# First weights in pieces of two row tiles, the last row tile in two column halves, a norm ahead of the gates

## The chip, the cores and the metric

The program runs on one core of a Trainium2 chip. A core has TensorE (matmuls), VectorE, ScalarE, GpSimd, and SyncE, which only issues transfers; the profile calls them PE (PEld for its weight loads), DVE, ACT, POOL and SP. Each takes its own instructions in order and waits on semaphores for the others. The metric is the device time of one execution in microseconds (us), as the median of several runs.

## The reference

One layer of a hybrid decoder on 1,024 prompt tokens and 8 x 8 sample tokens, all float32:

```python
h = rms_norm(x, norm_g)                          # over D_MODEL = 1024
a, gl, zc, q, k, v, zg, lr = split(h @ w_in)     # one projection
u  = a * sigmoid(gl)                             # 512 channels
cv = silu(group_layer_norm(causal_conv31(u)))
cv = (cv @ w_pw + b_pw) * silu(zc)
o  = gated_linear_attention(q, k, v, gate(lr))   # recurrent state, exact
o  = rms_norm_per_head(o) * silu(zg)
x  = x + concat(cv, o) @ w_out
y  = rms_norm(x, final_g)
```

The conv caches and the attention states are outputs too. In what follows only the first lines (norm, the projections `gl` and `a`) and the last two (`w_out`, residual, final norm) matter.

## The kernel before

**Layout.** The 1,088 tokens lie along the free dimension, in three chunks of 384, 384 and 320 tokens (`CHUNKS` 0, 1, 2); the 1,024 model channels lie in eight row tiles of 128 partitions (`x0` to `x7`). I call the chunks first, second and third by these numbers. The third is worked on first (`FIRST = 2`).

**Products.** A float32 product is made of three fast ones: each operand is split into a high part (a copy rounded by ScalarE: `hh` of x, `h_gl` and so on of weights) and a low part (the difference, by VectorE: `hl`, `l_gl`), and high x high, high x low and low x high are summed in PSUM. So a weight half (`s_gl0_0`: four row tiles by 128 columns, 256 KB) must be loaded, copied and subtracted before TensorE can use it. One projection of one column tile and one chunk is 8 row tiles x 3 = 24 matmuls.

**The start.** The parameters (`par`) are loaded first, then row tiles of the third chunk and halves of the first four weight tiles (`gl` and `a` for column tiles 0 and 1) in turn (L1004 to L1010). For the third chunk x is not normalised before the product: `raw_split` (L504) splits x times the norm's weights, and the result is scaled afterwards by `rs`, the norm factor of each token (`gl_chunk`, `early`). `rms_scale` (L513) makes that factor: squares `sq` on ScalarE, adds on VectorE, a matmul with a constant (`ms`) that sums over partitions, logarithm and exponential on ScalarE. `rms_split` (L530) applies it and splits; the first and second chunk go that way. Sigmoids need another function table on ScalarE than logarithm and exponential; a switch is an ACT_TABLE_LOAD.

**The end.** The product with `w_out` is done in seven products of half size (a Strassen-like scheme); the last, `pr4`, adds to four PSUM banks `acc` (`ya0` to `ya3`), one for each 128 tokens. `y_first` and `y_last` finish 128 tokens: square with a sum over columns, logarithm, exponential (the factor), then the two column halves are scaled, `y` on VectorE with the final weights and `z` on ScalarE, and both are stored by SyncE.

**What sets the order.** The code only lists operations. A planner (`schedule`) simulates the engines with estimated costs and latencies and emits each engine's instructions in the order of its simulation; among ready operations the one written first goes first. `late=True` ties a transfer to the last matmul written so far. Each pool has a fixed number of slots (`wst`, the staging of weights, has 4), and a transfer waits until the work on the slot's former tile is done. Transfers go through eight semaphores in turn, so that one waits for the eighth before it.

## Time and profile before

| | |
|---|---|
| median of three runs | 468.62 us (467.6 to 469.81) |
| the profiled execution, its own time | 470.14 us |
| its span, from first to last instruction | 468.4 us |
| mean granted clock of TensorE | 0.992 |
| TensorE / VectorE / ScalarE busy | 98% / 84% / 66% |

The span is shorter than the execution's time by 1.74 us, which lies around the instructions. Busy time of TensorE alone doesn't say that it works at its peak; the granted clock says at which of its two levels it ran (1.00 is 2.4 GHz).

### The profile page before, as it was taken

What the parts mean: (1) busy time and instruction counts of PE and PEld (TensorE: products, weight loads), DVE (VectorE), ACT (ScalarE), POOL (GpSimd) and SP (SyncE); (2) the same over time, 40 slices, a digit from 0 to 9 for tenths busy, and PEclk for the clock granted to TensorE, in tenths of its full rate; (3) what the DMA queues carried; (4) which work ended last, traced back from release to release, by engine and by line L of the source; (5) the groups of instructions that cost most, each with busy time, mean ns of one, the idle gap of its engine ahead of it and who ended that gap; (6) DMA issues with size and microseconds to landing.
All of it is one profiled execution on the core that took longest, in us unless ns stands there. A gap on an engine that the chain in (4) does not pass through costs nothing.

```text
span 468.4 us, 7544 instructions
## 1 busy us (share of the span) xinstructions
PE 457.8 (98%) x2714; PEld 420.8 (90%) x2714; DVE 393.4 (84%) x627; ACT 307.6 (66%) x769; POOL 19.8 (4%) x38
## 2 busy tenths in 40 slices
PE   7999999999999999999999999999999999999993
PEld 6899989999888899898999999999999988888782
DVE  4899997999999999998999999943538948998863
ACT  6897639974633624567766677653898648879735
POOL 1000000000000000000000000000000023130000
PEclk9999999999999999999999999999999999999998
DMA  8740273141300050002211121011235393385834
GB/s 250 265 146 7 88 167 50 45 59 56 58 0 1 8 171 1 2 22 92 69 57 45 41 97 45 24 59 65 81 78 182 88 226 58 77 180 138 288 127 179
DMA packets 35477, 43.26 MB, mean 92 GB/s; under 512 B 12912, under 2 KB 19824, under 8 KB 35440
## 3 DMA queue, kind: packets, MB, share of 16 engines
q1 hardware_dynamic: 33136, 38.59, 27.2%
q0 software_dynamic: 2304, 4.20, 5.5%
q8 instruction: 21, 0.34, 0.3%
q14 instruction: 16, 0.13, 0.1%
HBM read 36.58 MB, written 6.19 MB: 91 GB/s over the span
## 4 chain that ended last, share of the span: by engine, by line
PE 89%; ACT 3%; DMA 3%; DVE 2%; SPq 1%; issue 1%; DVEq 0%
PE p_zc L409 10%; PE pv L409 10%; PE p_zg L409 10%; PE p_gl L409 10%; PE p_a L409 9%; PE ya L409 7%; PE p_q L409 5%; PE p_k L409 5%; PE pw L409 5%; PE yc L409 5%; PE po L409 2%; PE pys L409 2%; SPq L397 1%; DMA s_gl<-in_w_in 1%; PE pa L409 1%; DMA xr<-in_x 1%
## 5 line engine op out<-in xcount | busy, mean ns | idle before, releaser
L359 DVE SCALAR_TENSOR_TENSOR cv<-u,par,cv 128x1024 f32<-128x1024 f32 x120 | 151.0, 1277 | 0.2
L409 PE MATMUL p_gl<-hh,h_gl 128*128 128x384 f32 (+1 forms) x96 | 32.5, 338 | 1.9 <-ACT h_gl L353 1.0
L353 ACT ACTIVATE pr<-us,par 128x64 f32<-128x64 f32 x124 | 31.9, 341 | 1.2 <-DMA us<-in_cc 1.2
L409 PE MATMUL p_gl<-hl,h_gl 128*128 128x384 f32 (+1 forms) x96 | 31.9, 332 | 0.1
L409 PE MATMUL p_gl<-hh,l_gl 128*128 128x384 f32 (+1 forms) x96 | 32.0, 333 | 0.0
L409 PE MATMUL p_a<-hh,h_a 128*128 128x384 f32 (+1 forms) x96 | 31.9, 332 | 0.0
L409 PE MATMUL p_a<-hl,h_a 128*128 128x384 f32 (+1 forms) x96 | 31.9, 332 | 0.0
L409 PE MATMUL p_a<-hh,l_a 128*128 128x384 f32 (+1 forms) x96 | 31.6, 331 | 0.0
L409 PE MATMUL p_zc<-hl,h_zc 128*128 128x384 f32 (+1 forms) x96 | 31.6, 329 | 0.0
L409 PE MATMUL p_zc<-hh,h_zc 128*128 128x384 f32 (+1 forms) x96 | 31.5, 328 | 0.0
L409 PE MATMUL p_zc<-hh,l_zc 128*128 128x384 f32 (+1 forms) x96 | 31.4, 328 | 0.0
L409 PE MATMUL p_zg<-hh,h_zg 128*128 128x384 f32 (+1 forms) x96 | 31.3, 326 | 0.0
L409 PE MATMUL p_zg<-hl,h_zg 128*128 128x384 f32 (+1 forms) x96 | 31.3, 326 | 0.0
L409 PE MATMUL p_zg<-hh,l_zg 128*128 128x384 f32 (+1 forms) x96 | 31.3, 326 | 0.0
L409 PE MATMUL pv<-h_v,hl 128*128 128x512 f32 x64 | 24.9, 390 | 0.0
L409 PE MATMUL pv<-l_v,hh 128*128 128x512 f32 x64 | 24.9, 389 | 0.0
L409 PE MATMUL pv<-h_v,hh 128*128 128x512 f32 x64 | 24.9, 389 | 0.0
L409 PEld LDWEIGHTS p_gl<-hh,h_gl 128*128 128x128 f32 x96 | 18.4, 191 | 3.0 <-ACT h_gl L353 1.5
L353 ACT ACTIVATE v<-pv 128x512 f32<-128x512 f32 x8 | 4.8, 599 | 21.9 <-PE pv L409 20.1
L409 PEld LDWEIGHTS p_gl<-hl,h_gl 128*128 128x128 f32 x96 | 18.5, 192 | 0.7 <-DVE hl L363 0.4
L409 PEld LDWEIGHTS p_gl<-hh,l_gl 128*128 128x128 f32 x96 | 18.3, 190 | 0.8 <-DVE cv L359 0.4
L363 DVE TENSOR_TENSOR o<-o,zg 128x384 f32<-128x384 f32 (+1 forms) x12 | 6.3, 533 | 14.7 <-ACT zg L353 14.7
(335 smaller groups left out, 1305.2 us busy)
## 6 DMA issues: line engine op xcount, KB each, us to landing
xr<-in_x SPq DMA_DIRECT2D x16, 256.0 KB, 4.1
out_y<-xr SPq DMA_DIRECT2D x16, 256.0 KB, 2.3
x<-in_xT SPq DMA_DIRECT2D x16, 192.0 KB, 4.1
T<-in_w_out POOLq DMA_DIRECT2D x12, 256.0 KB, 5.2
s_gl<-in_w_in SPq DMA_DIRECT2D x8, 256.0 KB, 5.1
s_a<-in_w_in SPq DMA_DIRECT2D x8, 256.0 KB, 3.9
s_v<-in_wv SPq DMA_DIRECT2D x16, 128.0 KB, 2.2
s_zc<-in_w_in SPq DMA_DIRECT2D x8, 256.0 KB, 3.0
```

The lines of the kernel that those rows point to most:

```text
L353: return S.activation(R(out), R(in_), func, **kw)
L359: return prog.add("DVE", lambda: V.scalar_tensor_tensor(R(out), R(a), R(s), R(b), op0, op1), [out], [a, s, b], out.n / 0.96 + 67 + 62 * is ...
L363: return prog.add("DVE", lambda: V.tensor_tensor(R(out), R(a), R(b), op), [out], [a, b], out.n / 0.96 + 67)
L397: prog.add("SP", lambda: nc.sync.dma_start(R(out), R(in_)), [out], [in_], 0, nbytes=v.n * 4 * (v.part[1] - v.part[0]))
L409: o = prog.add("PE", lambda: T.matmul(R(ps), R(lhsT), R(rhs), start=start, stop=stop, skip_group_check=True), [ps], [lhsT, rhs], c / share ...
```

## The change

Three parts. At the start, the four weight halves that hold row tiles 0 to 3 are loaded and converted in pieces of two row tiles (`whalf_parts`), and the parameters are loaded by ScalarE's queue. The first chunk's `rms_split` and the second chunk's `rms_scale` are written ahead of the third chunk's gates, and the third chunk's own split is held until the first chunk's first projection is done (`begun`). At the end, the product of the last 128 tokens is made in two column halves: the first in another bank (`acd[3]`, `yc3`), whose old sum in `acc[3]` is added to the residual beforehand; the tile's squares are summed in two parts; tile 6's `z` goes to VectorE; the last `z` is stored from ScalarE's queue. Besides, the planner has other estimates for transfers and early work, and one warm-up matmul less.

```diff
-NWARM = 10
+NWARM = 9
-        LAT = {..., "SP": 900}
+        LAT = {..., "SP": 700}
-            if same is not None and same.prio < best.prio + STICK:
+            if same is not None and t > SLACK_FROM and same.prio < best.prio + STICK:
-            if e == "SP":
-                t_free[e] = t + 60
-                dma[0] = max(dma[0], t) + 450
-                dma[1] = max(dma[1], dma[0] + 650) + o.bytes / 360.0
+            if e == "PE" and t < SLOW_TO:
+                cost *= 2
+            if o.bytes and e != "POOL":
+                t_free[e] = t + 450
+                dma_end = max(dma_end, t + 1000) + o.bytes / (250.0 if t < 4500 else 350.0)
...
-        def rms_split(c):
+        def rms_split(c, wait=None):
...
+                if wait is not None:
+                    prog.hold = wait
...
+        def whalf_parts(kind, i, h, stage=None):
+            name, src = f"{kind}{i}_{h}", A["w_in"][mt[(kind, i)]]
+            st = VT(stage or wst, "big" if stage else "wst", [P, 4, P], F32, f"s_{name}")
+            hi = VT(wh, "wh", [P, 4, P], F32R, f"h_{name}")
+            lo = VT(wl, "wl", [P, 4, P], F32R, f"l_{name}")
+            def piece(a, b, eng):
+                dma(st[:, a:b, :], src[:, 4 * h + a:4 * h + b, :], eng=eng)
+                split(hi[:, a:b, :], lo[:, a:b, :], st[:, a:b, :])
+            return (hi, lo), piece
...
-        dma(par, A["par"])
+        dma(par, A["par"], eng="ACT")
         w0, w1 = [[], []], [[], []]
         for h in range(2):
-            for i, (w, kind, ct) in enumerate(((w0[0], "gl", 0), ...)):
-                x_load(FIRST, range(4 * h + i, 4 * h + i + 1))
-                w.append(whalf(kind, ct, h, stage=big if 4 * h + i >= STAGE else None))
-                raw_split(range(4 * h + i, 4 * h + i + 1))
...
+            n = 2 if h == 0 else 4
+            for j in range(0, 4, n):
+                for i, piece in enumerate(parts_):
+                    if i < n:
+                        k = 4 * h + j + i
+                        x_load(FIRST, range(k, k + 1))
+                        raw_split(range(k, k + 1))
+                    piece(j, j + n, "SP")
         rms_scale(FIRST)
         x_load(0)
         x_load(1, late=True)
         rms_scale(0)
+        rms_split(0)
+        rms_scale(1)
         for ct, w in enumerate((w0, w1)):
             gl_chunk(ct, w[0], FIRST, True)
             a_chunk(ct, w[1], FIRST, True)
-        rms_split(0)
-        rms_scale(1)
         rms_split(1)
...
-        rms_split(FIRST)
+        rms_split(FIRST, begun)
...
+        def y_part(tk, y):
+            s_ = ss[tk]
+            y_square(tk, y, 4)
+            stt(s_[:, 1:2], s_[:, 4:5], 1.0 / DM, s_[:, 1:2], ALU.mult, ALU.add)
...
-            act(z, z, AF.Copy, scale=s_[:, 3:4])
+                ts(z, z, s_[:, 3:4], None, ALU.mult, None)
+            else:
+                act(z, z, AF.Copy, scale=s_[:, 3:4])
...
-        product(acc, pr4, False)
...
+        ends = [slice(0, 256), slice(256, 512)]
+        ys = [x_tile(4 + t, 0, mark) for t in range(4)]
+        tt(ys[3][:, ends[0]], acc[3][:, ends[0]], ys[3][:, ends[0]], ALU.add)
+        product(acc, pr4, False, range(3))
+        product(acd, pr4, True, [3], ends[0])
+        product(acc, pr4, False, [3], ends[1])
...
+        tt(ys[3][:, ends[0]], acd[3][:, ends[0]], ys[3][:, ends[0]], ALU.add)
+        y_part(7, ys[3][:, ends[0]])
+        o = tt(ys[3][:, ends[1]], acc[3][:, ends[1]], ys[3][:, ends[1]], ALU.add)
+        y_last(6, 0, o)
+        y_last(7, 0, None, ends[1], "ACT")
```

The first place in the order is SyncE's queue between the first chunk's last row tile and the second chunk's loads (`128x384` are x tiles of either chunk, `128x512` weight halves). Before:

```order
L397 DMA x6_112<-in_xT 128x384
L397 DMA x7_116<-in_xT 128x384
L397 DMA s_gl0_1_164<-in_w_in 128x512
L397 DMA s_a0_1_185<-in_w_in 128x512
L397 DMA s_gl2_0_203<-in_w_in 128x512
L397 DMA s_gl2_1_223<-in_w_in 128x512
L397 DMA s_a2_0_332<-in_w_in 128x512
L397 DMA x0_88<-in_xT 128x384
```

After:

```order
L402 DMA x6_176<-in_xT 128x384
L402 DMA x7_192<-in_xT 128x384
L402 DMA s_gl2_0_286<-in_w_in 128x512
L402 DMA s_gl2_1_296<-in_w_in 128x512
L402 DMA s_a2_0_323<-in_w_in 128x512
L402 DMA s_a2_1_343<-in_w_in 128x512
L402 DMA x0_88<-in_xT 128x384
L402 DMA x1_98<-in_xT 128x384
```

Two weight halves (`s_gl0_1`, `s_a0_1`) that stood behind the first chunk's x tiles have moved ahead of them, and `s_a2_1` now stands ahead of the second chunk's first x tile, not behind its last.

The second place is ScalarE where the first chunk is prepared: `rs0` is its norm factor, `sq1` are squares for the second chunk's norm, `hh` of 384 columns are the first chunk's high parts, those of 320 columns and `hp` the third chunk's. Before:

```order
L353 ACTIVATE rs0_352<-ms0_305,par_86 128x384
L353 ACTIVATE rs0_352<-rs0_352 128x384
L353 ACTIVATE hh0_143<-x0_88 128x320
L353 ACTIVATE hh1_151<-x1_92 128x320
L353 ACTIVATE hp_377<-hh0_143 128x64
L353 ACTIVATE sq1_0_382<-x0_88 128x384
L353 ACTIVATE hh0_143<-x0_88 128x384
L319 ACT_TABLE_LOAD
L353 ACTIVATE sig0_2_380<-sig0_2_380 128x320
L353 ACTIVATE hh1_151<-x1_92 128x384
```

After:

```order
L357 ACTIVATE rs0_380<-ms0_338,par_86 128x384
L357 ACTIVATE rs0_380<-rs0_380 128x384
L357 ACTIVATE sq1_0_390<-x0_88 128x384
L357 ACTIVATE sq1_1_397<-x1_98 128x384
L357 ACTIVATE hh0_114<-x0_88 128x384
L357 ACTIVATE sq1_2_407<-x2_116 128x384
L357 ACTIVATE hh1_130<-x1_98 128x384
L357 ACTIVATE hh2_172<-x2_116 128x384
L357 ACTIVATE sq1_3_423<-x3_127 128x384
L357 ACTIVATE hh3_194<-x3_127 128x384
```

The third chunk's high parts, the table load and its sigmoid are gone from between; the squares of row tiles 0 and 1 of the second chunk stand ahead of the first high part, those of 2 and 3 among the next.

The third place is VectorE at the end (`xr6_0` is the left half of tile 6, `ss` its sums and factor). Before:

```order
L363 TENSOR_TENSOR xr5_0_4757<-ya1_4216,xr5_0_4757 128x512
L359 SCALAR_TENSOR_TENSOR xr5_0_4757<-xr5_0_4757,ss5_4837,fg_4193 128x512
L363 TENSOR_TENSOR xr6_0_4759<-ya2_4233,xr6_0_4759 128x512
L363 TENSOR_TENSOR xr7_0_4761<-ya3_4247,xr7_0_4761 128x512
L359 SCALAR_TENSOR_TENSOR xr6_0_4759<-xr6_0_4759,ss6_4844,fg_4193 128x512
L359 SCALAR_TENSOR_TENSOR xr7_0_4761<-xr7_0_4761,ss7_4865,fg_4193 128x512
```

After:

```order
L367 TENSOR_TENSOR xr6_0_4778<-ya2_4246,xr6_0_4778 128x512
L367 TENSOR_TENSOR xr7_0_4801<-yc3_4489,xr7_0_4801 128x256
L363 SCALAR_TENSOR_TENSOR ss7_4870<-ss7_4870 128x1
L372 TENSOR_SCALAR xr6_1_4789<-xr6_1_4789,ss6_4861 128x512
L367 TENSOR_TENSOR xr7_0_4801<-ya3_4260,xr7_0_4801 128x256
L363 SCALAR_TENSOR_TENSOR xr6_0_4778<-xr6_0_4778,ss6_4861,fg_4203 128x512
L363 SCALAR_TENSOR_TENSOR xr7_0_4801<-xr7_0_4801,ss7_4870,fg_4203 128x512
```

Between tile 6's add and the last add stand the first half of tile 7, its sum, and the scaling of `xr6_1`, which was on ScalarE.

## Rows read from the trace of the kernel before

**Rows 1.** The page, part 1: busy us (share of the span) and instructions.

```profile
PE 457.8 (98%) x2714; PEld 420.8 (90%) x2714; DVE 393.4 (84%) x627; ACT 307.6 (66%) x769; POOL 19.8 (4%) x38
```

**Rows 2.** TensorE's waits, whole span: us in total, times, longest.

```profile
PE p_gl L409 <- ACT h_gl L353: 1.0, 1, 1.0
PE p_gl L409 <- ACT hh L353: 0.9, 1, 0.9
```

**Rows 3.** Stretches of the start: busy us and instructions, granted clock, DMA share, GB/s.

```profile
0.00:6.00 6.00, 4.93 (x21) 4.68 (x22) 1.08 (x3) 3.23 (x6) 1.97 (x11) 1.00 0.66 175
0.00:18.00 18.00, 15.04 (x73) 13.94 (x74) 10.92 (x22) 13.41 (x29) 1.97 (x11) 0.91 0.87 277
8.00:10.00 2.00, 0.41 (x1) 0.19 (x2) 0.57 (x2) 1.19 (x3) 0.00 (x0) 0.97 1.05 390
10.00:13.00 3.00, 3.00 (x11) 3.00 (x12) 2.82 (x6) 3.00 (x8) 0.00 (x0) 0.50 1.00 350
14.00:18.00 4.00, 4.00 (x29) 4.00 (x28) 3.65 (x8) 4.00 (x11) 0.00 (x0) 1.00 1.02 329
```

**Rows 4.** TensorE in order of time, 0 to 45 us: start, us, engine, line.

```profile
1.07 4.63 PE L409 MATMUL warm<-warm 128*128 128x128 f32 x20 [1.07 <-DVE warm L469]
...
5.66 0.64 PE L409 MATMUL p_gl<-hh,h_gl 128*128 128x320 f32 x1
...
27.44 0.34 PE L409 MATMUL p_gl<-hh,h_gl 128*128 128x384 f32 x1
...
30.50 0.44 PE L409 MATMUL p_gl<-hl,h_gl 128*128 128x384 f32 x1
```

**Rows 5.** All engines in order of time, the tail.

```profile
449.89 11.04 PE L409 MATMUL ya<-p4b,p4a 128*128 128x512 f32 x48
...
460.97 0.69 DVE L363 TENSOR_TENSOR xr<-ya,xr 128x512 f32<-128x512 f32 x1 [0.55 <-PE ya L409]
...
462.40 0.61 ACT L353 ACTIVATE sq<-xr 128x512 bf16<-128x512 f32 x1
...
463.14 0.53 ACT L353 ACTIVATE ss<-ss 128x1 f32<-128x1 f32 x2
...
463.70 0.75 DVE L359 SCALAR_TENSOR_TENSOR xr<-xr,ss,fg 128x512 f32<-128x512 f32 x1 [1.18 <-ACT ss L353]
464.45 0.81 SPq L397 DMA_DIRECT2D out_y<-xr  x2
```

**Rows 6.** ScalarE and VectorE in order of time, 0 to 32 us.

```profile
7.94 0.56 ACT L353 ACTIVATE hh<-x,par 128x320 fp32r<-128x320 f32 x1 [1.01 <-DMA x<-in_xT]
...
14.39 4.85 ACT L353 ACTIVATE sq<-x 128x320 f32<-128x320 f32 x12
...
23.54 0.53 ACT L353 ACTIVATE rs<-rs 128x384 f32<-128x384 f32 x1
...
25.46 0.51 ACT L353 ACTIVATE hh<-x 128x384 fp32r<-128x384 f32 x1
25.98 1.28 ACT L319 ACT_TABLE_LOAD   x1
...
29.90 1.95 DVE L363 TENSOR_TENSOR hl<-x,hh 128x384 fp32r<-128x384 f32 x4
```

**Rows 7.** The chain that ended last, 20 to 45 us.

```profile
39.19 3.30 PE p_gl L409 x19
```

**Rows 8.** SyncE's issues in order of time, the start.

```profile
1.19 0.42 SPq L397 DMA_DIRECT2D x<-in_xT  x1
...
7.93 0.33 SPq L397 DMA_DIRECT2D x<-in_xT  x1
...
20.97 4.23 SPq L397 DMA_DIRECT2D x<-in_xT  x8
```

**Rows 9.** VectorE's operations of line 369: duration ns min/median/max, first and last start.

```profile
L369 DVE TENSOR_SCALAR cv<-u,par x4: 806/808/810, 56.1 to 186.1; 128x1024 f32<-128x1024 f32 x4
```

**Rows 10.** Transfers from 455 us to the end, GB/s in 40 slices of 0.335 us.

```profile
GB/s 0 0 0 0 0 0 0 0 61 373 385 391 349 6 0 0 43 379 391 379 355 18 0 0 37 373 379 391 361 25 116 385 373 379 312 0 0 0 0 0
```

More of the change, by code (lines that the diff above doesn't have):

```diff
@@ L232, in cross @@
         def cross(d, o):
+            if d.eng == "ACT" and d.bytes:
+                return LAT["SP"] + IN[o.eng]
             if d.eng == o.eng:
@@ L269, in schedule @@
                 cost += 90
-            if e == "SP":
-                t_free[e] = t + 60
-                dma[0] = max(dma[0], t) + 450
-                dma[1] = max(dma[1], dma[0] + 650) + o.bytes / 360.0
-                o.end = dma[1]
+            if e == "PE" and t < SLOW_TO:
[3 more added lines that the diff above has]
+                dma_end = max(dma_end, t + 1000) + o.bytes / (250.0 if t < 4500 else 350.0)
+                o.end = dma_end
             else:
-                if e == "DVE":
+                if e == "DVE" and t > SLACK_FROM:
                     cost *= DVE_PACE
@@ L391, in zero, with dma @@
         fill(out, 0.0)
-    def dma(out, in_, late=False):
+    def dma(out, in_, late=False, eng="SP"):
         v = out if isinstance(out, View) else in_
@@ L396, in dma @@
             prog.hold = late
-        prog.add("SP", lambda: nc.sync.dma_start(R(out), R(in_)), [out], [in_], 0,
+        q = nc.sync if eng == "SP" else S
+        prog.add(eng, lambda: q.dma_start(R(out), R(in_)), [out], [in_], 0,
                  nbytes=v.n * 4 * (v.part[1] - v.part[0]))
@@ L481, in build, with x_load @@
         xs = {}
-        def x_load(c, ks=range(KT), late=False):
+        def x_load(c, ks=range(KT), late=False, eng="SP"):
             t0, n = CHUNKS[c]
@@ L486, in x_load @@
                 xk = rows("x", k, F32)[:, t0:t0 + n]
-                dma(xk, A["xT"][:, k, t0:t0 + n], late)
+                dma(xk, A["xT"][:, k, t0:t0 + n], late, eng)
                 xs[(c, k)] = xk
@@ L1200, in prep, with product @@
             return av, bv
-        def product(acc, ops, first):
+        def product(acc, ops, first, tiles=range(4), c=slice(0, 512)):
             av, bv = ops
-            for t in range(4):
+            for t in tiles:
                 ts_ = slice(P * t, P * t + P)
                 for k in range(4):
-                    mm(acc[t], av[k][:, 0, ts_], bv[k][:, 0, :], first and k == 0, False)
-                    mm(acc[t], av[k][:, 0, ts_], bv[k][:, 1, :], False, False)
-                    mm(acc[t], av[k][:, 1, ts_], bv[k][:, 0, :], False, k == 3)
+                    mm(acc[t][:, c], av[k][:, 0, ts_], bv[k][:, 0, c], first and k == 0, False)
+                    mm(acc[t][:, c], av[k][:, 0, ts_], bv[k][:, 1, c], False, False)
+                    mm(acc[t][:, c], av[k][:, 1, ts_], bv[k][:, 0, c], False, k == 3)
         pr1 = prep("p1", lambda i: A11[i], lambda i: B11("p", i))
@@ L1233, in y_first, with y_square, y_last @@
             ts(s_[:, 1:2], s_[:, 0:1], 1.0 / DM, eps[:rows_], ALU.mult, ALU.add)
[L1235 removed]
+        def y_square(tk, y, i):
+            junk = VT(unit, "unit", [P, 512], BF16, f"sq{tk}_{i}")[:y.part[1] - y.part[0], :y.n]
+            act(junk, y, AF.Square, accum=ss[tk][:, i:i + 1])
+        def y_part(tk, y):
+            s_ = ss[tk]
+            y_square(tk, y, 4)
+            stt(s_[:, 1:2], s_[:, 4:5], 1.0 / DM, s_[:, 1:2], ALU.mult, ALU.add)
+        def y_last(tk, h, after=None, part=None, eng="SP"):
             y, z, s_ = xr[(tk, h)], xr[(tk, 1 - h)], ss[tk]
             rows_ = y.part[1] - y.part[0]
[L1239 to L1240 removed]
+            y_square(tk, y if part is None else y[:, part], 2)
             act(s_[:, 3:4], s_[:, 2:3], AF.Ln, scale=1.0 / DM, bias=s_[:, 1:2])
@@ L1342, in build @@
             y_first(4 + t, 1)
-        product(acc, pr4, False)
-        for t in range(4):
-            y = x_tile(4 + t, 0, mark)
-            o = tt(y, acc[t], y, ALU.add)
-            if t == 3:
-                y_last(6, 0, o)
-            if t != 2:
-                y_last(4 + t, 0)
+        ends = [slice(0, 256), slice(256, 512)]
[4 more added lines that the diff above has]
+        product(acc, pr4, False, [3], ends[1])
+        for t in range(3):
+            tt(ys[t], acc[t], ys[t], ALU.add)
+            if t < 2:
+                y_last(4 + t, 0)
+        tt(ys[3][:, ends[0]], acd[3][:, ends[0]], ys[3][:, ends[0]], ALU.add)
[3 more added lines that the diff above has]
+        y_last(7, 0, None, ends[1], "ACT")
         with tc.manual_schedule():
```

24 lines of the change are left out of this document (14 added, 10 removed).

## The prediction

> **What bounds the kernel now.** I read the page first: TensorE is busy 457.8 of 468.4 us [rows 1]. Then its waits: only two between the first projection and the last product, 1.9 us together, both before 10 us [rows 2]. So the time is three pieces laid end to end: a start, until the engine is fed without a break; some 430 us of unbroken matmuls; and a tail after the last product. An edit pays only if it shortens the start or the tail, or leaves matmuls out; this change leaves none out.
>
> The start, by stretches [rows 3]: from 8 to 10 us the engine does one matmul, and from 10 to 13 it runs at a granted 0.50, the lower of its two levels (1.2 GHz), with 11 matmuls in 3 us where later 29 fit in 4 us at full clock. That loses 3 - 11 x 4/29 = 1.5 us. The first projection starts at 5.66, right behind the warm-up; the third chunk fills the time to 27.44, there the first chunk takes over, and at its 17th matmul (30.50) the engine has waited once more, for a low part from VectorE [rows 4]. From there it runs through.
>
> The tail: VectorE's add of the last tile begins at 460.97, the last two stores are issued from 464.45, the span ends at 468.4 [rows 5].
>
> **The change, part by part. (a) The loads in pieces.** On its own, TensorE could win the 1.9 us of waits, the 1.5 us of half clock and 0.4 us of warm-up (nine products instead of ten that take 4.63 us, [rows 4]): 3.8 us, the first chunk at 23.6. I don't book that, because the next late thing stands close behind it: the loads.
>
> The queue of after brings, up to row tile 1 of the second chunk: par 78 KB, eight x tiles of 164, eight weight halves of 262, eight x tiles of 197, four more weight halves, two x tiles of 197: 6,501 KB. In before, 277 GB/s over the first 18 us moved 4,986 KB, and from 14 to 18 us the rate is 329 [rows 3]. I take the same flow, since the DMA engines are busy 0.87 and more of it: the remaining 1,515 KB take 4.6 us, to 22.6. A load is usable later than its bytes: x2 of the third chunk was complete by bytes (1,094 KB; 1,050 by 6.0 us) at 6.1, and ScalarE, which waited for it, began at 7.94 [rows 3, 6], 1.8 us later. So that tile is usable at 24.4.
>
> This matters by the order of ScalarE: after puts the squares of row tiles 0 and 1 of the second chunk ahead of the first high part of the first chunk (the second place in the order). The squares pass one per 0.40 us (4.85 us for 12), a high part takes 0.51 [rows 6]: 24.4 + 0.4 + 0.5 = 25.3. The norm factor isn't what holds it: x7 of the first chunk comes by 5,059 KB, bytes at 18.2, usable at 20.0; then a square, an add, a sum matmul and two steps of ScalarE, some 0.5 us each, 22.5, against 24.07 in before [rows 6]. TensorE is not either: 23.6. So the first chunk starts at **25.3**, where before it started at 27.44, and its 17th matmul, at 0.174 us each (3.30 us for 19, [rows 7]), comes at 28.1 instead of 30.50: **2.4 us gained**. Bounds: with 277 GB/s instead of 329 it starts 0.9 later; with a shorter lag TensorE is the limit, 23.6. So 1.5 to 4.1.
>
> Then something new is late. All eight squares of the second chunk now precede high parts 4 to 7 of the first. Its x7 comes six tiles after x1 (1,180 KB, 3.6 us: 28.0), its square ends at 28.4, high part 4 at 28.9; behind it VectorE has eleven steps of some 0.49 us (1.95 us for four, [rows 6]) until the sums for the second chunk's norm are done, 34.3. TensorE reaches that sum after 52 matmuls, 9.0 us after 25.3: 34.3 too. Level by this count; with the steps' latencies **0.5 us of new wait**, bounds 0 and 1.
>
> What I cost at nothing: the parameters from ScalarE's queue (the first x tile is then SyncE's first issue instead of its second at 1.19 [rows 8]; should the parameters wait behind the first table load, the first conversion comes up to 0.6 us late). Four more conversions on ScalarE and four more subtractions on VectorE, about 0.1 us of fixed cost each. Both are covered by the loads, for which ScalarE waits from some 15 us on; uncovered they cost 0.6 and 0.4 us.
>
> **(b) The norm ahead of the gates** is what lets the first chunk begin that early: the table load (1.28 us, [rows 6]) and the two sigmoids that stood between its high parts now come behind all of them, and one switch serves instead of three. Its price is the waits above. The sigmoids come later, but nothing near waits for them: the second chunk's projections, which need their buffers, are over 15 us of matmuls away.
>
> **(c) The planner's other numbers.** The order behind 45 us is nearly the same one: a few neighbours swap. TensorE waits nowhere there now [rows 2]; zero, bounds -0.3 and +0.5.
>
> **(d) The last tile in two halves.** Tile 3 of product four becomes 24 matmuls of 256 columns. 512 columns pass in 0.227 us (11.04 us for 48, the last alone 0.39), 384 in 0.174 [rows 5, 7]; on that line 256 take 0.121, so 2.90 us instead of 2.72: **0.2 us lost** before the last add.
>
> After the last product, before: add 0.69; ScalarE is busy with tile 6 until 462.40; square to logarithm 0.74, logarithm to factor 0.56, scaling 0.75: stores from 464.45, 3.5 us after the add began [rows 5]. After: let A be the moment the second half can be added. The first half was ready 1.45 earlier; its add (0.42, a little over half of 0.69) and its square with read-out (0.6) end at A - 0.4 and stand, on ScalarE, between logarithm and exponential of tile 6. So tile 6's factor is there at A - 0.2, and VectorE scales that tile's other half next, which ScalarE did before. No row shows this operation's size; one of 1,024 columns takes 0.81 [rows 9], so 0.40 to 0.81, I take 0.54. The last add therefore starts at A + 0.35, not at A; add 0.42, square to logarithm 0.55 (0.2 less for half the columns), factor 0.56, scaling 0.75: stores at **A + 2.6**, both at once from two queues. The data then flow as before, two stores back to back at 370 to 390 GB/s [rows 10]. Gain **0.9 us**; bounds 1.2 (the scaling not in the way) and 0.2 (0.81 for it, and the second store 0.4 later).
>
> **Sum:** -2.4 + 0.5 + 0.2 - 0.9 = -2.6 us. The profiled execution has a span of 468.4 and a time of 470.14; the median of the three runs is 468.62, and the change is taken from that: 466.0.
>
> **A rule against the pieces.** In before, loads of 164 to 262 KB, up to eight under way (x7 goes out at 7.93, when x2, eight issues before it, is usable at 7.94 [rows 6, 8]), flow at 329 GB/s from 14 to 18 us [rows 3].
> The Trainium skill's "DMA: Bandwidth & Descriptors" (Rules for kernel authors) says to coalesce many small transfers into a large one; its bandwidth table has 0.95 us for 64 KB and 6.15 us for 1 MB, and on the line between them I estimate 1.3 us for 128 KB and 2.0 for 256, so that four halves cut in two would cost 4 x 0.6 = 2.4 us. By that rule the start's gain would be gone and 467.9 left.
>
> **Rivals.**
> *TensorE is the limit (0.18).* If a load's lag shrinks with smaller loads ahead of it, the first chunk starts at 23.6: 4.1 us gained at the start, no new wait, 0.7 in the tail: 463.8. For it: x7's bytes and the norm are there in time. Against: 6.5 MB must come through one queue.
> *The pieces cost flow (0.14).* Eight under way are 147 KB each instead of 213. If the time of one load stays and not the rate, the 1.7 MB of that stage take 7.5 us instead of 5.2 at 329 GB/s: up to 2.3 us, and all behind them as much later. With 1 to 2.3 us the result is 466.8 to 467.8. For it: the first 6 us move only 175 GB/s [rows 3]. Against: the first 2 us of these are empty, and later loads of 164 KB among them flow at full rate.
> *The clock falls in a wait (0.14).* The third chunk now has the sums of the first chunk's norm between its matmuls, and each waits for loads: by the count above some 1.7 us of waits before 25.3. In before, one matmul in 2 us was followed by 3 us at 0.50 [rows 3]. The same again loses 1.5 us: 467.5.
> *Slower: the second chunk's loads are held up (0.10).* On SyncE they now stand behind four weight halves, the last of which waits for a staging buffer that a subtraction on VectorE frees. In before they went out from 20.97 [rows 8] and nothing urgent waited; now ScalarE can't make the first high part without two of them. Each us by which the second of them is usable after 24.4 costs one us; at 27.0 the change is worth nothing, past 29.4 it is slower by over 0.5%; at 30 it is 471.6. For it: that weight half is itself among the last loads. Against: by bytes and lag it is there at 16.6, with 1.5 us of work behind it.
>
> **How the numbers follow.** The forecast, 466.0, has 0.44; its own bounds reach 464.8 to 467.2. A measurement of this kernel can tell about 0.5%, 2.3 us, from no change. The forecast lies just past that, so of its 0.44 I count 0.29 as faster; with TensorE as limit 0.18, and 0.05 of the two middling rivals: faster 0.52. Same: the rest of these, 0.38. Slower: 0.10. The range leaves out a tenth at either end: 463.7 to 468.4.
>
> **What would show it.** Right: the first chunk's first matmul at 24.4 to 26.2, ScalarE waiting for x ahead of it; clock 1.00 from 5 to 30 us; a short wait of TensorE at the second chunk's sum near 34; the last two stores issued together 2.6 us after the last product. Wrong: the first chunk waiting for the norm factor or for TensorE itself, a stretch at 0.50, a wait after 45 us, or a last add that starts at once.

## The result and the profile after

The changed kernel takes 474.17 us (median of four runs, 474.01 to 474.94) where the kernel before, measured beside it, takes 468.75: a ratio of 1.0124 (interval 1.0098 to 1.0150). The forecast was 466.0 with a range of 463.7 to 468.4: wrong in sign. The profiled execution of after took 474.28, its span is 472.5.

The page of after, its first line and part 1 (busy us, share of the span, instructions), against [rows 1]:

```profile
span 472.5 us, 7569 instructions
...
PE 455.3 (96%) x2724; PEld 418.8 (89%) x2724; DVE 394.4 (83%) x635; ACT 305.7 (65%) x772; POOL 19.5 (4%) x38
```

TensorE is busy 2.5 us less than before and the span is 4.1 us longer, so it stands still somewhere. Its waits in after (engine, line, waited for: us in total, times, longest; the warm-up's aside), where [rows 2] had two, both of the start:

```profile
PE pv L414 <- DVE l_v L367: 2.5, 1, 2.5
PE p_gl L414 <- ACT h_gl L357: 1.4, 2, 0.9
PE ya L414 <- DVE xr L367: 1.0, 1, 1.0
PE p_gl L414 <- ACT hh L357: 0.4, 1, 0.4
PE p_gl L414 <- DVE hl L363: 0.2, 1, 0.2
```

Two of these lie far behind 45 us, where the prediction had put zero: one at `pv`, the product with the attention's value weights, one at `ya`, the last product. The times at which TensorE reaches certain points show how much each stage weighs. `pl` is the first product behind the first and second chunk's projections, `p_q` begins the attention's, `p_zg` the projections behind it; the tail is from the first matmul of product four to the end of the span (e6 is an experiment below whose order is that of before up to the last tile):

| profile | `pl` | `pv` | `p_q` | `p_q` to `p_zg` | product four | tail | span |
|---|---|---|---|---|---|---|---|
| before | 65.0 | 113.9 | 161.6 | 139.0 | 449.9 | 18.5 | 468.4 |
| after | 63.8 | 112.7 | 163.2 | 137.3 | 449.3 | 23.2 | 472.5 |
| e6 | 64.0 | 112.9 | 160.6 | 139.1 | 448.6 | 18.2 | 466.8 |

From before to after: start -1.2, `pv` to `p_q` +2.8, `p_q` to `p_zg` -1.7, from there to product four -0.5, tail +4.7; together +4.1, the difference of the spans.

**The first loss.** Of after in order of time, ScalarE, VectorE and TensorE (start, us, engine, line, operation; in brackets the idle time and what ended it):

```profile
72.14 0.31 ACT L357 ACTIVATE Jr<-cst 128x128 fp32r<-128x128 f32 x1 [5.02 <-DMA cst<-in_cst]
...
73.97 0.38 ACT L357 ACTIVATE lr_h<-pl 128x272 fp32r<-128x272 f32 x1
...
74.38 0.44 DVE L367 TENSOR_TENSOR lr_l<-pl,lr_h 128x272 fp32r<-128x272 f32 x1 [4.13 <-ACT lr_h L357]
...
118.96 1.27 DVE L367 TENSOR_TENSOR l_v<-s_v,h_v 128x512 fp32r<-128x512 f32 x2
...
119.69 0.50 PE L414 MATMUL pv<-l_v,hh 128*128 128x512 f32 x1 [2.49 <-DVE l_v L367]
```

The same places of before:

```profile
70.39 0.31 ACT L353 ACTIVATE Jr<-cst 128x128 fp32r<-128x128 f32 x1 [3.44 <-DMA cst<-in_cst]
...
72.46 0.38 ACT L353 ACTIVATE lr_h<-pl 128x272 fp32r<-128x272 f32 x1
...
72.87 0.44 DVE L363 TENSOR_TENSOR lr_l<-pl,lr_h 128x272 fp32r<-128x272 f32 x1 [2.22 <-ACT lr_h L353]
...
116.21 0.69 DVE L363 TENSOR_TENSOR l_v<-s_v,h_v 128x512 fp32r<-128x512 f32 x1
...
118.21 0.39 PE L409 MATMUL pv<-l_v,hh 128*128 128x512 f32 x1
```

Read downward. ScalarE stands at a small conversion of constants (`Jr<-cst`) whose load hasn't landed: 3.4 us in before, 5.0 in after, where the load is issued 0.6 us later (one more piece of the value weights stands ahead of it on SyncE) and takes 1.1 us longer to land. Nothing needs the constants soon, but `lr_h` stands behind them on ScalarE, and VectorE stands behind `lr_h`. VectorE then has no idle time between 90 and 118 us in either profile, so what it has lost it never makes up: its 7th `l_v` begins 2.75 us later (1.5 from the constants, the rest from short waits for `h_v` and from two small steps put ahead of it). In before that tile was done at 116.9 and wanted at 118.2, a margin of 1.3 us. In after TensorE also comes 1.2 earlier: 2.75 + 1.2 - 1.3 = 2.65, and the wait is 2.5.

**The second loss**, of after in order of time, the tail's preparation and its end:

```profile
413.61 0.63 ACT L357 ACTIVATE s_b12u<-s_b12u 128x512 f32<-128x512 f32 x1 [2.49 <-DMA s_b12u<-in_w_out]
...
414.79 0.69 DVE L367 TENSOR_TENSOR p3a<-S,p3a 128x512 fp32r<-128x512 f32 x1 [4.19 <-ACT p3a L357]
...
453.22 5.74 PE L414 MATMUL ya<-p4b,p4a 128*128 128x512 f32 x24 [1.02 <-DVE xr L367]
...
460.24 1.60 PE L414 MATMUL ya<-p4b,p4a 128*128 128x256 f32 x12
...
466.37 0.41 DVE L367 TENSOR_TENSOR xr<-ya,xr 128x256 f32<-128x256 f32 x1
...
468.67 0.38 ACTq L402 DMA_DIRECT2D out_y<-xr  x1
```

The same pattern. A copy of `s_b12u` (a block of `w_out` for the seventh product, which is far off) has been placed ahead of `p3a` and `p3b`; its load was issued at 408.26 and the copy runs at 413.61. Before had it behind them, at 415.70; there the data had landed 1.3 us earlier, 5.5 us after the issue. The third product's operands, the finishing of other row tiles and their stores come later (first store 436.2, before 432.3), the residual's loads wait for those buffers (441.3, before 438.4), and at the end VectorE adds tile after tile 2.7 us apart. That is its pace in before too (each scaling waits for ScalarE's factor), so a late first tile makes the last one late. The last product ends at 461.8; the last add begins at 466.4, 4.5 us behind it. In before it began at once, and VectorE had waited only 0.55 us for it [rows 5].

### The profile page after: what moved, and what is told of

Its sections match the earlier page's. It is cut to its first block, busy times and chain, and to the rows that moved or that the text cites. A ratio compares the mean times of both kernels' runs of the same rounds, so it can differ in the third digit from the quotient of the medians.

```text
span 472.5 us, 7569 instructions
## 1 busy us (share of the span) xinstructions
PE 455.3 (96%) x2724; PEld 418.8 (89%) x2724; DVE 394.4 (83%) x635; ACT 305.7 (65%) x772; POOL 19.5 (4%) x38
## 4 chain that ended last, share of the span: by engine, by line
PE 68%; ACT 9%; DVE 9%; DMA 9%; issue 2%; SPq 1%; DVEq 0%; ACTq 0%
PE p_zc L414 10%; PE p_zg L414 10%; PE pv L414 9%; PE p_q L414 5%; PE p_k L414 5%; PE pw L414 5%; DVE cv L363 5%; PE ya L414 4%; PE p_gl L414 4%; PE p_a L414 4%; PE po L414 2%; ACT sq L357 2%; DMA xr<-in_x 2%; DMA x<-in_xT 2%; DVE xr L367 2%
## 5 line engine op out<-in xcount | busy, mean ns | idle before, releaser
L357 ACT ACTIVATE sq<-xr 128x512 bf16<-128x512 f32 (+2 forms) x19 | 11.4, 600 | 13.0 <-DVE xr L367 13.0
L414 PEld LDWEIGHTS p_zc<-hh,h_zc 128*128 128x128 f32 x96 | 18.0, 188 | 0.2 <-issue 0.2
```

What stands on the lines that cost most here:

```text
L357: return S.activation(R(out), R(in_), func, **kw)
L414: o = prog.add("PE", lambda: T.matmul(R(ps), R(lhsT), R(rhs), start=start, stop=stop, skip_group_check=True), [ps], [lhsT, rhs], c / share ...
```

## The experiments

The theory: because of the planner's new estimates for transfers two conversions in ScalarE's queue are reached ahead of the landing of their data, and these two places cost what the change lost. One, `s_b12u`'s, has moved forward in the queue; the other, the constants', stood ahead of its data in before too, and its load now comes later. The rivals: the tail's loss is the new tail's own (its chain through VectorE), the `pv` wait comes from the start. Ratios are to runs of before on the same chip.

**e1: the new estimates alone**, in before, with nothing else of the change.

```diff
-        LAT = {..., "SP": 900}
+        LAT = {..., "SP": 700}
...
-            if same is not None and same.prio < best.prio + STICK:
+            if same is not None and t > SLACK_FROM and same.prio < best.prio + STICK:
...
-                dma[0] = max(dma[0], t) + 450
-                dma[1] = max(dma[1], dma[0] + 650) + o.bytes / 360.0
+                dma_end = max(dma_end, t + 1000) + o.bytes / (250.0 if t < 4500 else 350.0)
...
```

> The kernel before with the planner's new estimates alone (transfer cost and latency, double cost of early matmuls, no grouping of matmuls before 45 us, VectorE's pace factor only after 45 us); its code is that of before. Theory A (two transfers that the new estimates put too early in ScalarE's order cost the time): ScalarE's copy of s_b12u0 stands ahead of p3's conversions as in after, and the time is 471 to 474, 3 to 5 us over before. Theory B (the last tile's halves and their early residual loads hold up VectorE): 468.2 to 469.2, like before. Theory C (TensorE's earlier start only runs into VectorE's limit): 468 to 469.

Measured: 476.4 us, 1.0183 (1.0145 to 1.0220). TensorE's late waits in it:

```profile
PE pv L411 <- DVE l_v L365: 3.9, 1, 3.9
...
PE ya L411 <- DVE xr L365: 0.9, 1, 0.9
```

Both late waits are there, and ScalarE waits 5.0 us for the constants and 2.7 at `s_b12u`, with the code of before's start and tail (the tail takes 21.7 us). The pieces and the halves aren't needed for the loss. The loss is even larger than the 3 to 5 us expected. The profiled execution is 10.6 us longer than before's: it loses 2.3 ahead of `pl` and 3.2 in the tail, and from `pv` to `p_q` it loses 5.8, of which 3.9 are the wait; behind the wait the granted clock is 0.50 (126 to 128 us).

**e2: the copies of `s_b12u` behind the third product's operands; e3: the constants loaded and converted early**, both on after; **e4: both.** The copies are held behind the last of the third product's conversions (`p3b3`), and the constants' block is moved up behind `gate_load`:

```diff
-        def t3(i):
-            return flip(B12("u", i), w_blk(4 + i, 1))
+        def t3(i, behind):
+            b = B12("u", i)
+            prog.hold = behind
+            return flip(b, w_blk(4 + i, 1))
...
+        behind = next(o for o in reversed(prog.ops) if o.eng == "ACT" and pr3[0][3].tile in o.tiles)
-        pr7 = prep("p7", s3, t3)
+        pr7 = prep("p7", s3, lambda i: t3(i, behind))
...
         w_rank = gate_load()
+        cst2 = un("cst2")
+        dma(cst2, A["cst2"], late=True)
+        for k_, t_ in enumerate((Jr, blkr, one_r)):
+            act(t_, cst2[:, k_ * P:(k_ + 1) * P], AF.Copy)
```

> After, with one dependency more: ScalarE's copies of s_b12u wait for the last conversion of p3, so that they stand behind p3's conversions as in before. TensorE's order is that of after, instruction for instruction. Theory A: ScalarE no longer waits 2.5 us for s_b12u0, VectorE no longer 4.2 us for p3a, the first stores go out near 432 instead of 436, TensorE's 1.0 us wait in the last product goes, the last add begins within 1 us of the last product: 468 to 469.5. Theory B: the residual loads still go out near 441 and the last add is still 4.5 us late: 473 to 474.

> After, with the three constant matrices (cst2) loaded and converted right behind the gate weights, near 35 us, instead of behind the conv caches. TensorE's order is that of after. Theory A: ScalarE's 5.0 us wait for cst goes, lr_h comes at 68 to 70 instead of 74, TensorE's 2.5 us wait for l_v at 117 goes; the tail's lateness stays, so 471.5 to 473. Theory C: VectorE is busy without a break from 88 us on in any case, so the wait goes but TensorE waits for VectorE elsewhere before 230 us: 473.5 to 474.5.

> After with both edits of the two runs before (constants early, s_b12u's copies behind p3's conversions). Theory A: both waits go and the forecast gains of start and tail come back: 465.5 to 467.5. Theory B: 471 to 473. Theory C: 468 to 469.5, as the copies alone.

Measured: e2 470.3 us, 1.0017 (0.9986 to 1.0047), tail 17.9. That is above the 468 to 469.5 expected. Its wait at `pv`, and a stretch behind it (us, busy us and instructions of PE, PEld, DVE, ACT and POOL, granted clock, DMA share, GB/s):

```profile
120.77 0.50 PE L414 MATMUL pv<-l_v,hh 128*128 128x512 f32 x1 [3.64 <-DVE l_v L367]
...
122.00:124.00 2.00, 2.00 (x6) 1.52 (x6) 1.94 (x3) 0.60 (x1) 0.00 (x0) 0.50 0.51 51
```

TensorE stands still for 3.6 us, and then the granted clock falls to 0.50, the lower level: six matmuls in 2 us where ten pass at 1.00. From `pv` to `p_q` e2's profile is 5.6 us longer than before's, 3.6 by the wait and 2.0 by the clock. Behind after's wait of 2.5 us the clock stayed at 1.00. Of e2's runs five have a mean granted clock of 0.995 or more and take 467.1 to 468.3 us, six have 0.993 or less and take 470.2 to 473.9; one run is profiled, so that the same fall makes the difference in the others isn't shown. e3 471.98, 1.0074 (1.0060 to 1.0087), no wait at `pv`, tail 22.5. e4 **466.18**, 0.9951 (0.9938 to 0.9965). Each edit cures its own wait and not the other. TensorE's waits in e4 (the warm-up's aside), again only of the start:

```profile
PE p_gl L414 <- ACT h_gl L357: 1.0, 1, 1.0
PE p_gl L414 <- ACT hh L357: 0.8, 1, 0.8
```

So the loss of the change is these two placements, and with both undone the rest of it is 0.5% ahead of before. The next runs ask which part of the rest does that.

**e5: e4 with before's tail; e6: before with after's tail.**

```diff
-        product(acc, pr4, False, range(3))
-        product(acd, pr4, True, [3], ends[0])
-        product(acc, pr4, False, [3], ends[1])
...
+        product(acc, pr4, False)
...
```

> e4_both with the tail of before: the last 128 tokens in one product of 512 columns, tile 6's z on ScalarE, both last stores from SyncE. TensorE's order is that of e4_both up to the last product. If the tail's halves are worth what was forecast (0.9 less 0.2): 466.8 to 467.0, 0.7 over e4_both. If they are worth nothing or cost: 465.7 to 466.3.

> The kernel before with the last tile's halves, y_part, tile 6's z on VectorE and the last z from ScalarE's queue; start, planner's estimates and order up to the last product as before. Theory A (order at fault, not the halves): 467.9 to 468.3, 0.7 under before; the last add begins 0.3 to 0.4 after it could. Theory B (the halves hold up VectorE): 470 or more.

Measured: e5 466.41, 0.9933 (0.9916 to 0.9951); e6 469.91, 1.0007 (0.9995 to 1.0019). The halves are worth nothing that these times can tell, either way. The end of e4, in order of time:

```profile
456.48 1.60 PE L414 MATMUL ya<-p4b,p4a 128*128 128x256 f32 x12
...
458.68 0.42 DVE L367 TENSOR_TENSOR xr<-ya,xr 128x256 f32<-128x256 f32 x1
...
460.99 0.38 ACTq L402 DMA_DIRECT2D out_y<-xr  x1
```

And of e5:

```profile
457.98 0.69 DVE L367 TENSOR_TENSOR xr<-ya,xr 128x512 f32<-128x512 f32 x1 [0.94 <-PE ya L414]
...
460.32 0.75 DVE L363 SCALAR_TENSOR_TENSOR xr<-xr,ss,fg 128x512 f32<-128x512 f32 x1 [0.99 <-ACT ss L357]
```

Both have product four's first matmul at 446.9. With halves the last product ends at 458.1, and the store goes out 2.9 us later; undivided the add begins at 457.98, and the scaling ends at 461.07, 3.1 us later. The halves win 0.2 and their matmuls cost 0.1. In before's own order (e6) the store goes out 3.0 us behind the last product where before needs 3.5 [rows 5], and the tail is 18.2 us where before has 18.5: 0.3 us, too little to show in the times.

e6 gave more than it was made for. Its instructions stand in the order of before on every engine up to the last tile, so its start is a second look at before's. A stretch of its start, which in [rows 3] is at 0.50:

```profile
10.00:12.00 2.00, 2.00 (x15) 2.00 (x15) 1.82 (x4) 2.00 (x6) 0.00 (x0) 1.00 1.02 313
```

And its first matmul of the first chunk, in order of time:

```profile
25.80 0.34 PE L412 MATMUL p_gl<-hh,h_gl 128*128 128x384 f32 x1
```

The half clock of [rows 3] is not in every execution. Without it before's own order starts the first chunk at 25.80, not 27.44 [rows 4], and reaches `pl` at 64.0, as e4 does.

**e7: after with the old transfer estimates from 45 us on**, and the constants' conversion behind `lr_h`.

```diff
+            if e == "SP" and t > EST_TO:
+                t_free[e] = t + 60
+                dma[0] = max(dma[0], t) + 450
+                dma[1] = max(dma[1], dma[0] + 650) + o.bytes / 360.0
+                o.end = dma[1] + 200
-            if o.bytes and e != "POOL":
+            elif o.bytes and e != "POOL":
...
```

> After with the transfer estimates of before from 45 us on and the constants converted behind lr_h: neither of the two waits, the tail's order as before, but among the attention's small matmuls TensorE's order goes back to that of before (31 changes between float32 and the fast kind from the q products to the zc products and 9 more behind them, as before, where e4_both has 24 and 2 to 20). Theory order: from the first q product to the first zg product it takes 139.0 us as in before, not the 137.3 of after and of e2 to e4, and the time is 467.6 to 468.4. Theory none (the 1.7 us come from elsewhere, as from transfers or VectorE): 137.3, and 465.8 to 466.6.

Measured: 469.89, 1.0005 (0.9988 to 1.0022). The late waits are gone but for 0.5 at `l_v`; the tail is 18.0; and yet it isn't e4, which has 0.9951. It reaches `pl` at 62.8, 1.2 us ahead of e4, and its span is 3.2 longer. Of these 4.4 us, 1.2 lie between `pv` and `p_q` (0.5 of it that wait) and 2.1 in the next stretch: `p_q` to `p_zg` takes 139.4 us, e4's 137.3. The first and last starts of these products' matmuls, in before:

```profile
L409 PE MATMUL p_q<-hh,h_q x48: 308/334/422, 161.6 to 216.8; 128*128 128x384 f32 x32, 128*128 128x320 f32 x16
...
L409 PE MATMUL p_zg<-hh,h_zg x96: 306/334/343, 300.6 to 353.0; 128*128 128x384 f32 x64, 128*128 128x320 f32 x32
```

And in e4:

```profile
L414 PE MATMUL p_q<-hh,h_q x48: 309/334/443, 160.6 to 215.8; 128*128 128x384 f32 x32, 128*128 128x320 f32 x16
...
L414 PE MATMUL p_zg<-hh,h_zg x96: 306/334/346, 297.9 to 350.0; 128*128 128x384 f32 x64, 128*128 128x320 f32 x32
```

Same work, no wait in either, 139.0 against 137.3 us. The order differs in how the attention's small float32 matmuls stand among those of the projections. My first theory was a price for each change between the two kinds: 50 changes in before and e7, 44 in e4.

**e8: e4 with whole weight halves** instead of the pieces.

```diff
-            n = 2 if h == 0 else 4
+            n = 4
```

> e4_both with the first weight halves loaded and converted whole (256 KB), not in pieces of two row tiles; the order ahead of 30 us follows from that, and the order of the attention's small matmuls goes back to that of before with it (1.7 us, see the stretch, not the total). Theory pieces: the first projection comes at 5.6 instead of 5.2, TensorE waits about 2 us before 11 us, a stretch at clock 0.50 comes back, the first chunk begins at 27.5 or later. Theory flow: the loads end when they end, the first chunk begins at 26.4 to 26.9 with or without pieces, behind ScalarE's wait for x.

Measured: 468.62, 0.9993 (0.9975 to 1.0010). Both theories had the first chunk at 26.4 or later, and both missed: in the start e8 is far ahead. e8 in two stretches, and its first matmul of the first chunk:

```profile
8.00:10.00 2.00, 2.00 (x15) 2.00 (x15) 2.00 (x5) 2.00 (x6) 0.00 (x0) 1.00 1.02 373
10.00:12.00 2.00, 2.00 (x16) 2.00 (x15) 2.00 (x5) 2.00 (x6) 0.00 (x0) 1.00 1.02 375
```

```profile
24.13 0.34 PE L414 MATMUL p_gl<-hh,h_gl 128*128 128x384 f32 x1
```

And after, with the pieces (e4, with the same pieces, has 225 and 323 GB/s in these stretches):

```profile
8.00:10.00 2.00, 2.00 (x16) 2.00 (x15) 2.00 (x6) 2.00 (x7) 0.00 (x0) 1.00 0.98 269
10.00:12.00 2.00, 2.00 (x16) 2.00 (x15) 1.96 (x6) 1.54 (x5) 0.00 (x0) 1.00 0.89 264
```

`pl` comes at 61.7 in e8, 64.0 in e4: 2.3 us. They are gone again at the end, because e8 has another order behind: `p_q` to `p_zg` 139.3 (50 changes), tail 18.8.

**e9: e8 with the planner's pace of VectorE at 1.03**, which gives 44 changes; **e10: e9 with `STICK = 250`**, which keeps TensorE longer at one kind: 36 changes.

```diff
-DVE_PACE = 1.05
+DVE_PACE = 1.03
...
-STICK = 60
+STICK = 250
```

> e8_whole_halves with one number of the planner changed (VectorE's pace factor 1.03 for 1.05), by which TensorE changes between float32 and the fast kind 44 times from the first q product to the first zg product, as in after and e2 to e5, not 50 as in before and e6 to e8. Theory changes (each costs some 0.3 us: 137.3 us for that stretch with 44, 139.0 to 139.4 with 50): 137.2 to 137.7 here, the first chunk at 24.1 to 24.6 as in e8_whole_halves, and the time 1.5 to 2 under e8's: 466.5 to 467.2, with the fastest runs near 465.3. Theory none: the stretch is at 139 and the time like e8's, 468.6.

> e9_whole_paced with the planner's readiness to stay with one kind of matmul raised (250 for 60): 36 changes in that stretch for 44. Theory changes: 8 x 0.3 less, 134.7 to 135.3 us for the stretch, and 2 to 2.6 under e9. Theory none, or the waits that staying brings eat it: 137 or more, and like e9 or slower.

Measured: e9 466.69, 0.9932 (0.9905 to 0.9959), stretch 137.7, `pl` 62.3. e10 469.3, 0.9996 (0.9973 to 1.0018), stretch 141.0. At a fixed price for each change 36 would have beaten 44. The 141.0 hold two other things: three waits of 0.2 to 0.3 us, and some 1.7 us for a fall of the clock, with TensorE busy throughout (e10, same columns as above):

```profile
260.00:262.00 2.00, 2.00 (x10) 2.00 (x9) 2.00 (x5) 1.01 (x2) 0.00 (x0) 0.50 0.00 0
```

Without them some 138.6 us are left, by estimate, and still not the 135.3 forecast at most: that theory falls.

**e11: before with the constants early and a pace of 1.04**; nothing of the change in it.

```diff
         w_rank = gate_load()
+        cst2 = un("cst2")
+        dma(cst2, A["cst2"], late=True)
...
-DVE_PACE = 1.05
+DVE_PACE = 1.04
```

> The kernel before with two edits: constants loaded and converted early (as in e3), and VectorE's pace factor in the planner 1.04 for 1.05, which gives 42 changes of kind for 50; start, halves and tail as before. Theory changes: the stretch takes 136.6 to 137.3 us for 139.0, and the time is 466.5 to 467.3. Theory start (the gain of e4 and e5 comes from the start): the stretch stays at 139 and the time at 468.5 to 469.5.

Measured: 467.1, 0.9937 (0.9914 to 0.9960), stretch 137.0 with 42 changes, `pl` 63.7. A gain like e4's is had with neither pieces nor halves. (Its tail takes 20.1 us, for a reason given at e13.)

**e12: e4 with the second chunk's squares held behind the second high part of the first chunk.**

```diff
+        for o in [o for o in prog.ops[mark_:] if o.eng == "ACT"][:8]:
+            o.deps.add(seen[SQ_AFTER])
```

> e4_both with the second chunk's squares on ScalarE behind the second high part of the first chunk (x0 and x1 of the second chunk no longer needed for the first one). The order of the attention's small matmuls goes back to 50 changes, 1.7 us, so the start alone is read. Theory squares: the first chunk begins at 25.6 to 25.9, 0.7 to 0.9 ahead of e4's 26.58, and ScalarE waits for no transfer ahead of it. Theory norm: it begins where VectorE has scaled the first row tile, 0.5 behind the norm factor, at 25.2 to 25.5 in e4, plus a high part: 25.8 to 26.2.

Measured: 468.53, 0.9981 (0.9964 to 0.9997); the first chunk starts at 25.94, e4's at 26.58, and `pl` is at 63.8 (64.0). ScalarE in e12, at the first high part:

```profile
25.32 1.58 ACT L358 ACTIVATE hh<-x 128x384 fp32r<-128x384 f32 x3 [0.69 <-DVE x L364]
```

So the squares hold the first chunk by 0.6 us, and what holds it next is the norm factor, ready at 24.6: ScalarE waits for VectorE to scale the first row tile with it, as the second theory had it. The stretch is 139.3 here too, which hides it in the total.

**e13: before with the small matmuls `pa` of two heads chained, so that they alternate; e14: e8 with the same.** Each `pa` uses 64 of the 128 rows, one head the upper, the other the lower. The order is the kernel's before but for one group and a few sums (`on`, `pvar`, `pj`) behind it: there, one head's last two stood in a row, then an `on`, then the other head's three.

```diff
+            n_wait = len(wait)
...
                 for j in range(2):
-                    mm(pa[j][:, s], km[HR[j], s], q[HR[j], s], True, True, wait, 2)
+                    wait = wait[:n_wait] + [mm(pa[j][:, s], km[HR[j], s], q[HR[j], s], True, True, wait, 2)]
```

> The kernel before, with the six small matmuls pa of each pair of heads chained so that the two heads alternate (each uses 64 of the 128 rows). Only one group changes its place: in before one head's last two stand in a row, then a sum (on), then the other head's three; now they alternate. Theory one head alone costs: in before's trace three such take 0.63 us and six (three of them in a row of one head) 0.87, where six that alternate take 0.55, so the stretch from p_q to p_zg falls from 139.0 to between 138.0 and 138.3, and the time by 0.7 to 1.0 us against before. Rival, the count of changes of kind (one fewer here): at 0.3 us for each, 138.7. Rival, nothing of this order matters and the 1.7 us lie elsewhere: 139.0.

> e8 (whole weight halves, constants early, copies behind) with the same chain. Theory one head alone costs: the stretch falls from 139.3 to between 138.3 and 138.7, the first chunk stays near 24.1 and the time falls from 468.6 to about 467.8, a ratio near 0.997. Rival nothing of this order matters: 139.3 and a ratio near 0.999.

Measured: e13 468.8, 0.9982 (0.9966 to 0.9998), stretch **138.0**; e14 466.34, 0.9933 (0.9915 to 0.9950), where e8 had 0.9993; stretch 137.8, first chunk 24.23, span 462.8. The place in before, in order of time (the trace has two records for each `pa`; the expectation above took each record for a matmul):

```profile
217.01 0.94 PE L409 MATMUL pa<-ge,g 64*128 64x128 f32 x12
...
221.17 0.71 PE L409 MATMUL pa<-ge,g 64*128 64x128 f32 x4
221.80 0.44 PE L409 MATMUL on_0p<-on_0l,one_r 128*128 128x384 f32 x1
222.17 0.93 PE L409 MATMUL pa<-ge,g 64*128 64x128 f32 x6
223.04 0.44 PE L409 MATMUL on_0p<-on_0h,one_r 128*128 128x384 f32 x1
```

And in e13:

```profile
221.27 0.82 PE L409 MATMUL pa<-ge,g 64*128 64x128 f32 x9
```

Six alternating `pa` (x12) take 0.77 us from their start to the next operation's. Five that stand by head take 0.63 + 0.87 = 1.50 in before, and some 0.6 in e13. The starts of single records show how: with the heads in turn two records, one of each head, begin 0.007 us apart and the next two 0.11 later; by head each begins 0.11 behind the one before. By the difference of starts, all `pa` of the stretch take 5.2 us in before and 4.3 in e13 and e4; that is 0.9 of the 1.7, and the sums and `px` have most of the rest. In all profiles, those with the heads apart have 139.0 to 139.4 in this stretch (e10, with the clock and waits named there, 141.0), those that alternate 137.0 to 138.0.

In e13's profile the 1.0 us doesn't reach the end. Product four begins at 448.4 where before has 449.9, but the tail takes 19.9 us instead of 18.5, and the span is 468.3. VectorE at the last two tiles of e13:

```profile
459.66 1.28 DVE L363 TENSOR_TENSOR xr<-ya,xr 128x512 f32<-128x512 f32 x2
```

It makes the last add right behind the one before it, 0.9 us after the product's end. In before VectorE had 0.55 us in hand there [rows 5]; once TensorE is ahead by more, VectorE's chain of 2.7 us for each tile sets the end. e11 ends in the same way, with its 20.1 us. e14 keeps its gain: of the 2.7 us between its span and e8's, 1.5 are the stretch and 1.1 the tail, which nobody forecast.

## Why the prediction was wrong, point by point

**The step that failed** is part (c): "TensorE waits nowhere there now [rows 2]; zero, bounds -0.3 and +0.5." An engine that never waits was read as an engine with slack behind it. What had to be looked at is the margin of those that feed it: at `pv` VectorE was 1.3 us ahead, and at `s_b12u` the data had landed 1.3 us ahead of ScalarE's copy. "A few neighbours swap" was true, and two of the swaps were these: a copy of `s_b12u` with the third product's conversions, a piece of the value weights with the constants' load. Measured: 2.5 us at `pv` and 4.7 in the tail, against -1.7 and -0.5 of the middle's order, which were not forecast either: 0.9 of the 1.7 is two heads' `pa` standing in turn again (e13). e1 shows the losses without the rest of the change, e4 the rest without the losses. The planner now counts a 256 KB load as usable 2.45 us after its issue (1.0 + 0.75 + 0.7 by its formulas; before 2.7); the trace of after took 5.3 for `s_b12u`. Both formulas were too short, and in before the order happened to fit the landings.

**(a) The start.** The path was the right one, but only just: ScalarE waits for x ahead of the two squares and the first high part. Of after in order of time:

```profile
24.01 0.52 ACT L357 ACTIVATE rs<-rs 128x384 f32<-128x384 f32 x1
...
24.83 1.07 ACT L357 ACTIVATE sq<-x 128x384 f32<-128x384 f32 x2 [0.30 <-DMA x<-in_xT]
25.81 0.51 ACT L357 ACTIVATE hh<-x 128x384 fp32r<-128x384 f32 x1
...
26.36 0.44 PE L414 MATMUL p_gl<-hh,h_gl 128*128 128x384 f32 x1 [0.37 <-ACT hh L357]
```

The tile was usable 0.4 later than the 24.4 forecast, and two squares followed where one was counted; first chunk at 26.36, not 25.3. The norm factor, which the sum had at 22.5 and so out of the way, is there at 24.5, and ScalarE's wait for x behind it is 0.3 us; e12 shows that it holds the first chunk as soon as the squares are gone. The new wait of 0.5 at the second chunk's sum didn't come. Net, by `pl`: 1.2 us instead of 1.9, against the profiled execution. Against e6's profile of the same order at full clock it is 0.2. So the base was mis-sized too: 27.44 comes 1.6 us behind e6's 25.80 (1.0 by `pl`), and the half clock lies between. The fixed cost of a further piece, put at about 0.1 us, is 0.18 on ScalarE and 0.15 on VectorE in after (two of 0.40 for one of 0.62, two of 0.42 for one of 0.69), off the path either way. The sum was made against that execution's 470.14 and its change carried over to the median, 468.62.

**The rule against the pieces** had the direction right, and my rejection of it was wrong. Here the pieces move 225 to 323 GB/s between 8 and 14 us in e4, the whole halves 362 to 375 in e8, and the first chunk starts 2.45 us earlier. The Trainium skill's "DMA: Bandwidth & Descriptors" (Rules for kernel authors) says to coalesce many small transfers, and warns of those under 64 KB; the trace agrees for pieces of 128 KB. The estimate from its table was 2.4 us, of times of single transfers added up; that the 2.45 measured lies so near isn't shown to be more than chance. I had set against it that later loads of 164 KB flow at full rate, but these are among loads of 262 KB, so what counts may be the mean size under way, which no run tests alone. SyncE's pace isn't what held the pieces: by 8 us e4 had issued 2.27 MB, of which 1.57 had moved (by the rates to 8 us, an estimate). That is the rival "the pieces cost flow" (0.14). Its 466.8 to 467.8 don't follow from its own 1 to 2.3 us, which added to 466.0 give 467.0 to 468.3.

**(b) The norm ahead of the gates** cost what was forecast, nothing: no wait of TensorE on it, at `ms` or at a gate.

**(d) The tail.** The mechanism came as told: the last add is held, by 0.6 instead of 0.35, because tile 6's scaling stands ahead of it, and the two stores go out together. The size was off: stores at 2.9 us after the product instead of 2.6 (e4), and in e4's order the base isn't 3.5. Of the 3.5, 0.4 is ScalarE busy with tile 6 in before's order; e5, undivided, needs 3.1. The 0.9 shrinks to 0.2, less 0.1 for the matmuls; in before's own order it is 0.5, and the tail gains 0.3 (e6).

**The other rivals.** "TensorE is the limit" and "the clock falls in a wait" did not occur in after: x comes at 24.8, and the granted clock is 1.00 throughout the start. In e1 and e2 the clock did fall, behind the waits at `pv`. "Slower" had 0.10 through the second chunk's loads; these came in time, and the slowness came by a way that no rival named.

**That e4 lands on 466.2**, beside the forecast, is chance: against e6 its start gains nothing and its tail 0.3, and product four begins 1.7 us earlier, for which the middle's order has 1.8.

**Open:** some 0.6 us of the middle's 1.7 (e13 and e14 stand at 138.0 and 137.8, e4 at 137.3), which the sums between the projections may have; why e1's start is 2.3 us later than before's (in its profile the clock falls a second time, between 27 and 31 us); and why the clock falls in one execution and not in the next.

## What to carry to other kernels

An engine without waits says nothing of the margin of the engines that feed it: before an edit that moves instructions is costed at zero, read for each moved conversion when its data land and who stands behind it in the same queue, and for the next engine how far ahead of its consumer it is. The same margin bounds a gain: TensorE's 1.0 us in e13 ended at a VectorE that was 0.55 us ahead. When a planner's estimates change, every in-order queue of the program changes with them; try the estimates apart from the edit they were made for. And a price read from one execution is to be seen in a second one before it is carried to a median.

## What the runs showed of the hardware that was not expected

- The clock at the start differs between executions of one order: 0.50 from 10 us in the profiled execution of before [rows 3], 1.00 in e6. In 69 runs of before beside e1 to e12, the 32 with a mean granted clock of 0.995 or more have a median of 468.6 us, the 25 with 0.992 or less 469.95. It also fell to 0.50 behind waits of 3.6 and 3.9 us at `pv` (e2, e1), not behind one of 2.5 (after), and once in e10 at 260 us with TensorE busy.
- Weight loads of 128 KB in place of 256 KB, from one queue with several under way, flow at 225 to 323 GB/s where the larger ones flow at 362 to 375 (8 to 14 us).
- Small matmuls on 64 of the 128 rows, from two heads in turn, take 0.13 us each (0.77 for six); by head, one behind the other, 0.3 (1.50 for five). In turn, the records of the two heads begin in pairs, 0.007 us apart. The profile shows no wait in either.
